# Queries and first expert groups of the latent routing as plain fp32 products, weights left unsplit, in a two-layer network on one core

## The chip, the cores and the metric

The kernel runs on one core of one Trainium2 chip. The metric is the device time of one execution in microseconds (us), from the device's own clock; lower is better. The runs of the kernel before took 4352.44 us in the median (3 runs, 4348.89 to 4359.93).

## The reference, cut to what matters

The program is a chain of mixers and feed-forward blocks on 256 latent rows and 256 context rows of width 1024. The part that the change touches is the expert layer, called twice on the latents (layers 0 and 1 of the second block):

```
def peer(x [256 x 1024], w_query, sub_keys, u, v):
    qry = (x @ w_query) as 8 heads x 2 halves x 128
    s   = qry . sub_keys            # 128 keys per head and half
    the 16 best of each half, their 256 sums, the 16 best of those
    idx, gate = expert numbers and softmax of the 16 best, per row and head
    act  = gelu(x . u[idx])         # 16384 experts, as 128 groups of 128
    return sum(gate * act * v[idx])
```

All of it is fp32 in the reference.

## The kernel before, in words

**Split products.** TensorE has a one-pass form for 32-bit operands of reduced precision (`fp32r`). To keep fp32 accuracy the kernel splits every operand x into hi = x rounded to that form (ACT, line 221) and lo = x - hi (VectorE "DVE" or GpSimd "POOL", line 222), and makes three products hi*hi, hi*lo and lo*hi (`mm3`, lines 224 to 228). Weights come as 512 KB loads into one of five raw buffers (`wraw`, tag of lines 355 and 356), and their parts go to five `whi` and four `wlo` buffers. `unit` (line 325) loads and splits a block of weights, `unit32` (line 342) loads it and leaves it unsplit. A product of unsplit fp32 operands shows in the trace as two matmul records, and a split product as three.

**The latent expert layer, `peer_lat` (line 2029), for each of two layers.**
1. `norm_T` (line 438) normalises the 256 rows, transposes them on TensorE into the tile `nfull`, and splits that into the pair `plhh`, `plhl` (named hT), 4 column blocks of 128 at a time.
2. `route` (line 1736), eight heads. For each: load 128 keys (`skT`), load and split two halves of query weights, 16 split products of 128x256 into PSUM, copy (`qry`, line 1752), four key products in plain fp32 (`at`, line 1757), copy (`tks`, line 1759), and four `top16` on DVE (lines 1829 to 1837). `skT` and the four scratch tiles `t16` of the `top16` of a head share one pool tag of four buffers (line 156, "s1").
3. `topk` (line 1768), twice, all on DVE: sums of the candidates (line 1787), 8 `top16`, and two look-ups (lines 1809 to 1811) over 128x1024 elements.
4. `build_G` (line 1926): 64 steps, each with DVE comparisons (lines 1954 and 1961), four plain fp32 products (line 1964) and a copy (line 1965), then stores of the gate matrix to DRAM.
5. The dense stretch: for each of 128 groups the split of u (on DVE) and of v (ACT, POOL), 24 products for x.u (128x256) and 12 of 128x512 for the sum over v, into PSUM (lines 2023 to 2025).

**The groups ahead.** Beside steps 2 to 4 the first `backlog` groups of step 5 have their x.u computed in advance (`ahead`, line 2083): 20 in layer 0 and 36 in layer 1. Each loads a 512 KB block of u (`dense_w`, line 1970), splits it with the lower part on POOL (since `a_mod` and `a_pool` are 1), makes 24 split products (`dense_u`, line 1981) and applies gelu.

**What sets the order.** The kernel is traced in program order, and a scheduler then orders each engine's queue by a simulated timeline: the earliest-written instruction whose inputs and buffers are ready goes first. `lockstep` and `idle` place the groups ahead behind the heads in program order (`u_lag` is 18 steps, and the eight heads are 16), but the scheduler lifts them forward where an engine is idle. In layer 0 the expert work of the context rows runs in the background: row gathers by POOL (line 1883) and weighted sums on DVE (lines 1906 and 1912).

Of the kernel before, what the change touches and what calls it, by code (L numbers as in the profile page):

```python
# [9 lines left out]
F32 = mybir.dt.float32  # L10
# [3 lines left out]
AF = mybir.ActivationFunctionType  # L14
# [6 lines left out]
P = 128  # L21
# [3 lines left out]
def ds(a, n):  # L25
    return slice(a, a + n)
# [72 lines left out]
class Builder:  # L99
# [242 lines left out]
    def unit32(self, ap, kk=KD):  # L342

        n = ap.n
        src = ap.parts(kk)
        nh = len(src)
        kh = kk // nh
        raws = []
        for i in range(nh):
            raws.append(self.w_raw()[:, :kh * n].rearrange("p (k c) -> p k c", k=kh))  # L350
            self.load(raws[i], src[i])
        self.tick()
        return Rows(raws, kh)

    def w_raw(self, name="wraw"):
        return self.pw.tile([P, 1024], F32, name=name, tag="wraw", bufs=self.n_raw)
# [78 lines left out]
        self.rstd(ss[:, 1:2], ss[:, 0:1], n)  # L435
        return ss[:, 1:2]

    def norm_T(self, x, ntile, gcol, sc, sh, hT, t0, pool, keep=None):
        nc = self.nc
        gs = self.t_([P, KD], "gs")  # L440
        nc.vector.scalar_tensor_tensor(gs, sc, 1.0, gcol, op0=ALU.add, op1=ALU.mult)
        xn = []
        for t in range(ntile):
            r = self.row_rstd(x[:, t], 1024)
            y = self.t_([P, 1024], "xn")
            nc.vector.tensor_scalar(y, x[:, t], r, None, op0=ALU.mult)
            xn.append(y)
        nt = ntile * P
        for k2 in range(0, KD, 4):
            whole = not isinstance(hT, tuple)  # L450
            full = hT[:, ds(k2, 4), ds(t0, nt)] if whole else self.t_([P, 4, nt], "nfull")
            for k1 in range(0, 4, 2):
                ps = self.ps_tr([P, 2, nt])
                for k in range(2):
                    for t in range(ntile):
                        nc.tensor.transpose(ps[:, k, ds(t * P, P)], xn[t][:, ds((k2 + k1 + k) * P, P)], self.ident)
                for k in range(2):
                    kk = k2 + k1 + k
# [43 lines left out]
class Block1:  # L502
# [101 lines left out]
    def out_res(self, yT, kt, W, gbc, x):  # L604
        nc = self.nc
        groups = [(k, min(KD, kt - k)) for k in range(0, kt, KD)]
        for cb in range(0, 1024, 512):
            ps = [self.ps_mm([P, 512], name="orp") for _ in range(2)]
            for gi, (k0, kk) in enumerate(groups):
                for h in range(2):  # L610
                    w = self.unit(W[k0 * P:(k0 + kk) * P, cb + h * 256:cb + h * 256 + 256], kk)
                    for t in range(2):
                        hv = (yT[0][:, ds(k0, kk)], yT[1][:, ds(k0, kk)])
                        self.xs(ps[t][:, ds(h * 256, 256)], hv, t * P, w, 0, 256, kk,
                                start=gi == 0 and h == 0, stop=gi == len(groups) - 1 and h == 1)
# [239 lines left out]
    def transp_split(self, y, nk, yT, nt, t0=0):  # L855

        nc = self.nc
        for k0 in range(0, nk, 2):
            ps = self.ps_tr([P, 2, nt * P])
            for k in range(2):  # L860
                for t in range(nt):
                    nc.tensor.transpose(ps[:, k, ds(t * P, P)], y[:, t, ds((k0 + k) * P, P)], self.ident)
            self.split(yT[0][:, ds(k0, 2), ds(t0, nt * P)], yT[1][:, ds(k0, 2), ds(t0, nt * P)], ps)

    def attn_tiles(self, pm):
        nc, A = self.nc, self.A
# [848 lines left out]
class Peer:  # L1715
# [2 lines left out]
    s_mod, s_pool = 4, 0  # L1718
    g_mul, g_mod = 0, 4
    mod_r, s_lag, s_eng = 0, 3, "DVE"  # L1720
    bg_r, bg_dense, bg_ahead, a_mod, a_pool, u_lag, u_route = 0.0, 1.4, 1.0, 1, 1, (18, 18), (18, 20)

    def peer_const(self):
        nc, pc = self.nc, self.pc
# [11 lines left out]
    def route(self, layer, hT, T, out):  # L1736


        nc, A = self.nc, self.A
        code, gate = T("code", [P, 2, 8, 16]), T("gate", [P, 2, 8, 16])  # L1740
        tk = T("tk", [P, 2, 2, 16, 16])
        v1, iu = tk[:, 0], tk[:, 1].bitcast(U32)
        sk = A["peer_sub_keys_2"][layer]
        for h in range(8):
            skT = self.t_([P, 2, P], "skT")
            self.load(skT, sk[h])
            w = self.unit(A["peer_w_query_2"][layer][:, h * 256:h * 256 + 256])
# [12 lines left out]
            for t in range(2):  # L1760
                for c in range(2):
                    self.top16(v1[:, t, 2 * h + c], iu[:, t, 2 * h + c], sc[:, t, c])
            yield
        out += [code, gate]
        for t in range(2):
            yield from self.topk(v1[:, t], iu[:, t], code[:, t], gate[:, t], T)
# [200 lines left out]
                yield  # L1967
            nc.sync.dma_start(self.d_G[:, :, ds(t0, n)], Gs)

    def dense_w(self, layer, g, D, pool=False):  # L1970

        u = self.w_raw("ur")
        self.load(u, self.A["peer_u_2_T"][layer, g])
        uh, ul = self.w_hi("uh"), self.w_lo("ul")
        self.split(uh, ul, u, pool)
        v = lambda t: t.rearrange("p (k c) -> p k c", k=8)
        D["uhl", g] = v(uh), v(ul)

    x_lead = 2

    def dense_u(self, layer, g, hT, D):

        nc = self.nc
        uh, ul = D.pop(("uhl", g))
        pa = self.psu.tile([P, 256], F32, name="pact", bufs=2)
        for k in range(8):
            self.mm3(pa, uh[:, k], ul[:, k], hT[0][:, k], hT[1][:, k], k == 0, k == 7)
        ge = self.pge.tile([P, 256], F32, name="ge", bufs=self.backlog[layer] + 2)
        nc.scalar.activation(ge, pa, AF.Gelu)  # L1989
        D[g] = ge  # L1990
# [38 lines left out]
    def peer_lat(self, layer, x, mod, gcol, fill=None):  # L2029

        nc = self.nc
        self.es_ps.close()
        B = self.backlog[layer]
        with ExitStack() as es:
# [5 lines left out]
            with ExitStack() as esr:  # L2040
# [1 line left out]
                self.n_mm, self.n_tr, self.n_at = 2, 1, 1  # L2042
                pr = self.pool(esr, f"rt{layer}", "right")
                self.lo_pat = "d"
                self.norm_T(x, 2, gcol, mod[:, 32:40, 0], mod[:, 24:32, 0], hT, 0, ph)
                gbc = self.gate_bc(mod, 5, 0, ph, "plg")
                res = []
                u = self.ahead(layer, hT, D)
                tag = lambda name: dict(tag="Gs", bufs=2) if name == "eq" else dict(tag=name, bufs=1)
                T = lambda name, shape: pr.tile(shape, F32, name=name, **tag(name))  # L2050
                fill = fill or iter(())
                self.bg_rate = self.bg_r if layer == 0 else 0.0
                self.lockstep(self.route(layer, hT, T, res), chain(islice(self.idle(), 8), self.spread(islice(fill, self.mod_r), 1)), chain(islice(self.idle(), self.u_lag[layer]), islice(u, self.u_route[layer])))
                self.bg_rate = 0.0
                self.lockstep(self.build_G(res[0], res[1], pr), self.spread(chain(u, fill), self.g_spread))
                for _ in fill:
                    pass
            self.psc = self.pool(es, f"psc{layer}", psum=True)
            pv = self.pool(es, f"pv{layer}", "right")
            pacc = self.pool(es, f"pacc{layer}", "right", psum=True)  # L2060
# [22 lines left out]
    def ahead(self, layer, hT, D):  # L2083
        n = self.backlog[layer]
        for g in range(n):
            for i in range(g + 1 if g else 0, g + 2):
                if i < n:
                    self.dense_w(layer, i, D, i % self.a_mod < self.a_pool)
            self.dense_u(layer, g, hT, D)
            self.bg(self.bg_ahead)  # L2090
            yield
# [204 lines left out]
```

## Time and profile before

| what | value |
|---|---|
| median of 3 runs | 4352.44 us |
| the profiled execution, its own time | 4345.28 us |
| its span, first to last instruction | 4343.6 us |
| mean granted TensorE clock | 0.894 of full |
| busy: TensorE, weight load, DVE, ACT, POOL | 81%, 73%, 70%, 45%, 49% |
| layer 0: heads, topk, `build_G`, dense | from 2221, 2314, 2402, 2546 us |
| layer 1: heads, topk, `build_G`, dense | from 3405, 3493, 3585, 3728 us |

Times inside the profile are counted from the start of its span. PE is TensorE's matmul and PEld its weight load. A matmul record lasts longer than the step to the next, since matmuls are pipelined, so the step between starts is what a product costs in a row of products.

### The profile page before, as it was taken

The numbers are of one execution on the slowest core, as the hardware profiler recorded it, in microseconds if no ns is written. First come the engines' busy times: TensorE is split into PE (matmuls) and PEld (weight loads), VectorE is DVE, ScalarE is ACT, GpSimd is POOL, SyncE is SP. The second block draws the span as 40 slices with busy tenths as digits, with TensorE's granted clock in tenths as the row PEclk, the third lists the DMA queues.
The fourth block names the chain that finished last, engine by engine and source line by source line (L and its number), as shares of the span: only waits on it lengthen the run. The fifth ranks groups of instructions, "written<-read, shape, count | busy, mean of one in ns | idle before, by whom it ended". The sixth has DMA issues, their size and how long they took to land. (4 is left out here: it accounts for less than half of the span.)

```text
span 4343.6 us, 68593 instructions
## 1 busy us (share of the span) xinstructions
PE 3525.7 (81%) x25277; PEld 3153.0 (73%) x25277; DVE 3039.7 (70%) x5920; ACT 1936.6 (45%) x3523; POOL 2126.1 (49%) x1632
## 2 busy tenths in 40 slices
PE   6788779697777864676586779999978878899998
PEld 4667768585677864566486668988857878799997
DVE  3745457876779986877668977888895599544435
ACT  3355444245344443244233345555545434455555
POOL 1233312453466764667716058888863161444444
PEclk8788889788888987888788999999999989999999
DMA  7586443663677887888755779999872345666655
GB/s 281 173 237 192 119 156 131 234 222 135 216 276 252 278 288 223 277 268 247 241 208 176 242 252 340 331 325 326 325 244 89 119 138 182 220 207 216 208 175 184
DMA packets 424010, 972.05 MB, mean 224 GB/s; under 512 B 70322, under 2 KB 211834, under 8 KB 418938
## 3 DMA queue, kind: packets, MB, share of 16 engines
q1 hardware_dynamic: 349946, 699.20, 49.4%
q0 software_dynamic: 73728, 268.47, 17.7%
q8 instruction: 199, 3.26, 0.3%
q14 instruction: 137, 1.12, 0.1%
HBM read 898.66 MB, written 68.88 MB: 223 GB/s over the span
## 5 line engine op out<-in xcount | busy, mean ns | idle before, releaser
L222 POOL TENSOR_TENSOR vl<-vr,vh 128x512 fp32r<-128x512 f32 x460 | 652.7, 1437 | 584.4 <-ACT vh L221 580.0
L226 PE MATMUL pact<-plhh,uh 128*128 128x256 f32 x2048 | 584.6, 285 | 31.4 <-ACT ge L1989 31.3
L227 PE MATMUL pact<-plhl,uh 128*128 128x256 f32 x2048 | 584.7, 285 | 0.0
L228 PE MATMUL pact<-plhh,ul 128*128 128x256 f32 x2048 | 584.5, 285 | 0.0
L221 ACT ACTIVATE whi<-wraw 128x1024 fp32r<-128x1024 f32 (+1 forms) x350 | 366.6, 1050 | 398.1 <-PE mm L227 115.0
L1883 POOL DMA_INDIRECT sg<-in_peer_u_dram,sidx x256 | 332.3, 1298 | 296.8 <-DVE sg L1906 190.0
L222 DVE TENSOR_TENSOR wlo<-wraw,whi 128x1024 fp32r<-128x1024 f32 (+1 forms) x256 | 327.7, 1284 | 181.8 <-ACT whi L221 89.4
L1912 DVE SCALAR_TENSOR_TENSOR spy<-sg,sact,spy 128x1024 f32<-128x1024 f32 x254 | 429.1, 1689 | 20.4 <-DMA sg<-in_peer_v_dram,sidx 19.1
L1883 POOL DMA_INDIRECT sg<-in_peer_v_dram,sidx x256 | 336.9, 1316 | 208.8 <-DVE spy L1912 113.4
L1906 DVE SCALAR_TENSOR_TENSOR sg<-sg,sph 128x1024 f32<-128x1024 f32 x256 | 381.3, 1500 | 79.0 <-DMA sg<-in_peer_u_dram,sidx 78.6
L2024 PE MATMUL acc<-vl,ch 128*128 128x512 f32 x1024 | 407.6, 398 | 26.7 <-POOL vl L222 18.3
L226 PEld LDWEIGHTS pact<-plhh,uh 128*128 128x128 f32 x2048 | 395.8, 193 | 42.8 <-ACT ge L1989 32.6
L227 PEld LDWEIGHTS pact<-plhl,uh 128*128 128x128 f32 x2048 | 395.7, 193 | 10.4
L2025 PE MATMUL acc<-vh,cl 128*128 128x512 f32 x1024 | 400.9, 391 | 0.0
L228 PEld LDWEIGHTS pact<-plhh,ul 128*128 128x128 f32 x2048 | 395.5, 193 | 4.3 <-POOL ul L222 0.2
L221 ACT ACTIVATE uh<-ur 128x1024 fp32r<-128x1024 f32 x256 | 271.1, 1059 | 264.0 <-PE pact L227 182.3
L2023 PE MATMUL acc<-vh,ch 128*128 128x512 f32 x1024 | 357.2, 395 | 30.1 <-ACT vh L221 30.1
L222 POOL TENSOR_TENSOR wlo<-wraw,whi 128x1024 fp32r<-128x1024 f32 (+1 forms) x94 | 233.2, 2491 | 298.1 <-PE mm L228 74.6
L221 ACT ACTIVATE vh<-vr 128x512 fp32r<-128x512 f32 x512 | 307.6, 624 | 117.5 <-PE acc L2025 100.2
L222 DVE TENSOR_TENSOR ul<-ur,uh 128x1024 fp32r<-128x1024 f32 x200 | 282.5, 1413 | 109.0 <-PE pact L228 104.7
L2004 DVE TENSOR_TENSOR cl<-co,ch 128x256 fp32r<-128x256 f32 x256 | 107.6, 420 | 217.7 <-ACT ch L2003 215.8
L2000 DVE TENSOR_TENSOR co<-co,G 128x256 f32<-128x256 f32 x256 | 167.3, 654 | 121.9 <-ACT co L1999 98.3
(647 smaller groups left out, 10116.7 us busy)
## 6 DMA issues: line engine op xcount, KB each, us to landing
ur<-in_peer_u_T_dram SPq DMA_DIRECT2D x256, 512.0 KB
vr<-in_peer_v_dram SPq DMA_DIRECT2D x256, 512.0 KB
wraw<-in_ada_w_dram SPq DMA_DIRECT2D x96, 512.0 KB
wraw<-in_dn_w_in_dram SPq DMA_DIRECT2D x96, 512.0 KB
wraw<-in_w_in_dram SPq DMA_DIRECT2D x64, 512.0 KB
d_G<-Gs SPq DMA_DIRECT2D x32, 1024.0 KB
G<-d_G SPq DMA_DIRECT2D x32, 1024.0 KB
wraw<-in_w_mod_dram SPq DMA_DIRECT2D x48, 512.0 KB
```

The source lines that it names most:

```text
L221: nc.scalar.activation(hi, src, AF.Copy)
L222: (nc.gpsimd if pool else nc.vector).tensor_tensor(lo, src, hi.bitcast(F32), ALU.subtract)
L226: mm(out, lh, rh, start=start, stop=False)
L227: mm(out, lh, rl, start=False, stop=False)
L228: mm(out, ll, rh, start=False, stop=stop)
L1883: nc.gpsimd.indirect_dma_start(out=g, out_offset=None, in_=A[tab][0], in_offset=bass.IndirectOffsetOnAxis(ap=self.s_idx[:, t, j:j + 1], ax ...
L1906: nc.vector.scalar_tensor_tensor(g, g, 1.0, h, op0=ALU.mult, op1=ALU.mult, accum_out=act[:, j:j + 1])
L1912: nc.vector.scalar_tensor_tensor(y, g, act[:, j:j + 1], y, op0=ALU.mult, op1=ALU.add)
L2000: nc.vector.tensor_tensor(co, co, D["G"][:, :, g % 8], ALU.mult)
L2023: mm(acc[t][h], ch[:, tt], vh[h], start=first, stop=False)
L2024: mm(acc[t][h], ch[:, tt], vl[:, hh], start=False, stop=False)
L2025: mm(acc[t][h], cl[:, tt], vh[h], start=False, stop=last)
```

## The change

It does four things, in `peer_lat` alone:
- `norm_T` writes the unsplit transposed rows into two tiles `plf` (named hf) taken from the four `wlo` buffers, instead of the scratch `nfull`. The pair hT is still split from it, for the dense stretch.
- `route` and `ahead` get hf instead of hT. So the queries and the groups ahead load their weights unsplit and make one plain fp32 product where three split products stood.
- While `wide` is 2 (from the norm to the end of `build_G`) unsplit loads take turns between the `wraw` and the `whi` buffers, ten instead of five.
- Groups ahead are loaded three ahead instead of one (`a_lead`), without any split.

Branches for an unsplit input are also added to `out_res` and `transp_split`; their callers still hand in pairs. The context's routing (`peer_ctx`) also hands in a pair. The core of the diff:

```diff
+    wide, wide_i = 1, 0
+    def raw32(self):
+        tags = (("wraw", self.n_raw), ("whi", self.n_hl), ("wlo", self.n_lo))[:self.wide]
+        self.wide_i += 1
+        tag, n = tags[self.wide_i % len(tags)]
+        return self.pw.tile([P, 1024], F32, name="wraw", tag=tag, bufs=n)
...
     def unit32(self, ap, kk=KD):
-            raws.append(self.w_raw()[:, :kh * n].rearrange("p (k c) -> p k c", k=kh))
+            raws.append(self.raw32()[:, :kh * n].rearrange("p (k c) -> p k c", k=kh))
...
     def norm_T(...):
-            full = hT[:, ds(k2, 4), ds(t0, nt)] if whole else self.t_([P, 4, nt], "nfull")
+            full = (hT if whole else plain)[:, ds(k2, 4), ds(t0, nt)] if whole or plain is not None else self.t_([P, 4, nt], "nfull")
...
     def route(...):
-            w = self.unit(A["peer_w_query_2"][layer][:, h * 256:h * 256 + 256])
+            w = (self.unit if isinstance(hT, tuple) else self.unit32)(A["peer_w_query_2"][layer][:, h * 256:h * 256 + 256])
...
-    def dense_w(self, layer, g, D, pool=False):
-        u = self.w_raw("ur")
+    def dense_w(self, layer, g, D, whole=False):
+        v = lambda t: t.rearrange("p (k c) -> p k c", k=8)
+        u = self.raw32() if whole else self.w_raw("ur")
         self.load(u, self.A["peer_u_2_T"][layer, g])
+        if whole:
+            D["u", g] = v(u)
+            return
...
     def dense_u(self, layer, g, hT, D):
         for k in range(8):
-            self.mm3(pa, uh[:, k], ul[:, k], hT[0][:, k], hT[1][:, k], k == 0, k == 7)
+            if isinstance(hT, tuple):
+                self.mm3(pa, u[0][:, k], u[1][:, k], hT[0][:, k], hT[1][:, k], k == 0, k == 7)
+            else:
+                nc.tensor.matmul(pa, u[:, k], hT[:, k], start=k == 0, stop=k == 7)
...
     def peer_lat(...):
-                self.norm_T(x, 2, gcol, mod[:, 32:40, 0], mod[:, 24:32, 0], hT, 0, ph)
+                hf = Rows([self.pw.tile([P, 4, 256], F32, name="plf", tag="wlo", bufs=self.n_lo) for _ in range(2)], 4)
+                self.norm_T(x, 2, gcol, mod[:, 32:40, 0], mod[:, 24:32, 0], hT, 0, ph, plain=hf)
+                self.wide = 2
...
-                u = self.ahead(layer, hT, D)
+                u = self.ahead(layer, hf, D)
...
-                self.lockstep(self.route(layer, hT, T, res), ...)
+                self.lockstep(self.route(layer, hf, T, res), ...)
...
+            self.wide = 1
...
     def ahead(self, layer, hT, D):
-            for i in range(g + 1 if g else 0, g + 2):
+            n_x = self.a_lead
+            for i in range(g + n_x if g else 0, g + n_x + 1):
                 if i < n:
-                    self.dense_w(layer, i, D, i % self.a_mod < self.a_pool)
+                    self.dense_w(layer, i, D, True)
```

## Rows read from the trace of the kernel before

**Rows 1.** Busy time by stretch: us, PE, PEld, DVE, ACT, POOL, PEclk, DMA share, GB/s.
```profile
2314.00:2402.00 88.00, 38.47 (x304) 36.70 (x302) 86.54 (x257) 17.48 (x28) 44.45 (x26) 0.74 0.52 168
...
2546.00:3140.00 594.00, 580.54 (x3616) 519.58 (x3617) 494.23 (x487) 316.65 (x621) 518.13 (x351) 1.00 0.90 327
3405.00:3493.00 88.00, 80.51 (x634) 78.65 (x632) 49.85 (x238) 40.30 (x55) 25.48 (x11) 0.95 0.46 139
3493.00:3585.00 92.00, 63.50 (x493) 62.89 (x492) 91.44 (x225) 32.15 (x46) 54.80 (x21) 0.85 0.38 124
3585.00:3728.00 143.00, 110.60 (x859) 103.88 (x858) 125.31 (x338) 58.19 (x95) 12.52 (x5) 0.95 0.62 188
3728.00:4300.00 572.00, 571.19 (x3472) 513.91 (x3473) 245.03 (x343) 324.04 (x645) 277.54 (x215) 0.99 0.62 208
```

**Rows 2.** Timeline of one head in layer 1: start us, us, engine, line, operation.
```profile
3473.55 0.60 ACT L1759 ACTIVATE tks<-at 128x512 f32<-128x512 f32 x1 [0.20 <-PE at L1757]
...
3474.18 0.87 DVE L1832 MAX8 tk<-tks 128x8 f32<-128x128 f32 x4 [4.74 <-ACT tks L1759]
...
3478.25 0.33 SPq L168 DMA_DIRECT2D skT<-in_peer_sub_keys_dram  x1
...
3481.51 1.06 PE L1757 MATMUL at<-skT,qry 128*128 128x128 f32 x8
...
3482.86 0.59 ACT L1759 ACTIVATE tks<-at 128x512 f32<-128x512 f32 x1
```

**Rows 3.** The score copies of the eight heads, layer 0 then layer 1.
```profile
L1759 ACT ACTIVATE tks<-at x8: 581/599/599, 2242.4 to 2313.7; 128x512 f32<-128x512 f32 x8
...
L1759 ACT ACTIVATE tks<-at x8: 581/597/599, 3424.6 to 3492.4; 128x512 f32<-128x512 f32 x8
```

**Rows 4.** Groups of 3405 to 3493: busy us, mean ns, idle before and releasers.
```profile
L226 PE MATMUL mm<-plhh,whi 128*128 128x256 f32 x128 | 37.9, 299 | 4.2 <-ACT plhh L221 2.2 <-ACT qry L1752 2.0
...
L226 PE MATMUL pact<-plhh,uh 128*128 128x256 f32 x60 | 17.1, 286 | 0.0
...
L222 DVE TENSOR_TENSOR wlo<-wraw,whi 128x1024 fp32r<-128x1024 f32 x12 | 14.6, 1216 | 9.0 <-PE mm L228 7.9 <-ACT whi L221 1.1
```

**Rows 5.** TensorE's timeline near 2303 us, layer 0.
```profile
2302.58 0.28 PE L226 MATMUL pact<-plhh,uh 128*128 128x256 f32 x1
2302.70 0.28 PE L227 MATMUL pact<-plhl,uh 128*128 128x256 f32 x1
...
2302.94 1.06 PE L1757 MATMUL at<-skT,qry 128*128 128x128 f32 x8
```

**Rows 6.** DVE's groups of the topk stretch of layer 1, 3493 to 3585.
```profile
L1809 DVE TENSOR_TENSOR eq<-tkpf,iotaf 128x1024 f32<-128x1024 f32 x4 | 13.6, 3436 | 0.1
L1810 DVE TENSOR_TENSOR eq<-eq,tk 128x1024 f32<-128x1024 f32 x4 | 11.3, 2860 | 0.0
...
L1810 DVE TENSOR_TENSOR eq<-eq,cand 128x1024 f32<-128x1024 f32 x4 | 8.7, 2202 | 0.0
L1787 DVE TENSOR_TENSOR cand<-tk 128x64 f32<-128x64 f32 (+3 forms) x10 | 7.9, 823 | 0.0
L1817 DVE SCALAR_TENSOR_TENSOR cand<-cand 128x128 f32<-128x128 f32 x2 | 4.9, 2448 | 0.1
L1809 DVE TENSOR_TENSOR eq<-tkpf,starts 128x1024 f32<-128x1024 f32 x4 | 4.7, 1218 | 0.0
L1774 DVE CAST tk<-tk 128x256 f32<-128x256 uint32 x2 | 4.0, 2022 | 0.0
...
L1818 DVE TENSOR_TENSOR tkpf<-tkpf,cand 128x128 f32<-128x128 f32 x2 | 0.6, 292 | 0.1
```

**Rows 7.** DVE's groups of the topk stretch of layer 0, 2314 to 2402.
```profile
L1787 DVE TENSOR_TENSOR cand<-tk 128x64 f32<-128x64 f32 (+3 forms) x10 | 8.0, 835 | 0.0
L1810 DVE TENSOR_TENSOR eq<-eq,cand 128x1024 f32<-128x1024 f32 x4 | 6.9, 1759 | 0.0
...
L1822 DVE TENSOR_TENSOR tkex<-tkb 128x128 f32<-128x128 f32 x2 | 2.7, 1350 | 0.0
```

More of the change, by code (lines that the diff above doesn't have):

```diff
@@ L436, in row_rstd, with norm_T @@
         return ss[:, 1:2]
-    def norm_T(self, x, ntile, gcol, sc, sh, hT, t0, pool, keep=None):
+    def norm_T(self, x, ntile, gcol, sc, sh, hT, t0, pool, keep=None, plain=None):
         nc = self.nc
@@ L610, in out_res @@
                 for h in range(2):
-                    w = self.unit(W[k0 * P:(k0 + kk) * P, cb + h * 256:cb + h * 256 + 256], kk)
+                    both = isinstance(yT, tuple)
+                    w = (self.unit if both else self.unit32)(W[k0 * P:(k0 + kk) * P, cb + h * 256:cb + h * 256 + 256], kk)
                     for t in range(2):
-                        hv = (yT[0][:, ds(k0, kk)], yT[1][:, ds(k0, kk)])
+                        hv = (yT[0][:, ds(k0, kk)], yT[1][:, ds(k0, kk)]) if both else yT[:, ds(k0, kk)]
                         self.xs(ps[t][:, ds(h * 256, 256)], hv, t * P, w, 0, 256, kk,
@@ L862, in transp_split @@
                     nc.tensor.transpose(ps[:, k, ds(t * P, P)], y[:, t, ds((k0 + k) * P, P)], self.ident)
-            self.split(yT[0][:, ds(k0, 2), ds(t0, nt * P)], yT[1][:, ds(k0, 2), ds(t0, nt * P)], ps)
+            if isinstance(yT, tuple):
+                self.split(yT[0][:, ds(k0, 2), ds(t0, nt * P)], yT[1][:, ds(k0, 2), ds(t0, nt * P)], ps)
+            else:
+                nc.scalar.activation(yT[:, ds(k0, 2), ds(t0, nt * P)], ps, AF.Copy)
     def attn_tiles(self, pm):
@@ L1720 @@
     mod_r, s_lag, s_eng = 0, 3, "DVE"
-    bg_r, bg_dense, bg_ahead, a_mod, a_pool, u_lag, u_route = 0.0, 1.4, 1.0, 1, 1, (18, 18), (18, 20)
+    bg_r, bg_dense, bg_ahead, u_lag, u_route = 0.0, 1.4, 1.0, (18, 18), (18, 20)
     def peer_const(self):
@@ L1968, in build_G @@
             nc.sync.dma_start(self.d_G[:, :, ds(t0, n)], Gs)
-    def dense_w(self, layer, g, D, pool=False):
-        u = self.w_raw("ur")
+    def dense_w(self, layer, g, D, whole=False):
+        v = lambda t: t.rearrange("p (k c) -> p k c", k=8)
+        u = self.raw32() if whole else self.w_raw("ur")
         self.load(u, self.A["peer_u_2_T"][layer, g])
+        if whole:
+            D["u", g] = v(u)
+            return
         uh, ul = self.w_hi("uh"), self.w_lo("ul")
[L1975 to L1979, printed above, removed]
+        self.split(uh, ul, u)
+        D["u", g] = v(uh), v(ul)
+    x_lead, a_lead = 2, 3
     def dense_u(self, layer, g, hT, D):
         nc = self.nc
-        uh, ul = D.pop(("uhl", g))
+        u = D.pop(("u", g))
         pa = self.psu.tile([P, 256], F32, name="pact", bufs=2)
         for k in range(8):
-            self.mm3(pa, uh[:, k], ul[:, k], hT[0][:, k], hT[1][:, k], k == 0, k == 7)
+            if isinstance(hT, tuple):
+                self.mm3(pa, u[0][:, k], u[1][:, k], hT[0][:, k], hT[1][:, k], k == 0, k == 7)
+            else:
+                nc.tensor.matmul(pa, u[:, k], hT[:, k], start=k == 0, stop=k == 7)
         ge = self.pge.tile([P, 256], F32, name="ge", bufs=self.backlog[layer] + 2)
@@ L2052, in peer_lat @@
                 self.bg_rate = self.bg_r if layer == 0 else 0.0
-                self.lockstep(self.route(layer, hT, T, res), chain(islice(self.idle(), 8), self.spread(islice(fill, self.mod_r), 1)), chain(islice(self.idle(), self.u_lag[layer]), islice(u, self.u_route[layer])))
+                self.lockstep(self.route(layer, hf, T, res), chain(islice(self.idle(), 8), self.spread(islice(fill, self.mod_r), 1)), chain(islice(self.idle(), self.u_lag[layer]), islice(u, self.u_route[layer])))
                 self.bg_rate = 0.0
```

## The prediction

> **What bounds the kernel now.** I read the split by stretch first, then the timeline and the groups of each stretch. The two dense stretches hold more than half of the span after 2221 us, and PE is busy there for 580.5 of 594 us and 571.2 of 572 us [rows 1]. The change leaves their products alone, so a dense stretch that begins earlier ends earlier by as much. What can move is the part ahead of each: heads, topk and `build_G`.
>
> In the heads neither DVE (49.9 of 88 us) nor POOL is full [rows 1]. One head costs a chain, seen whole in one turn [rows 2]: scores copied at 3473.55, `top16` from 3474.18, and the keys of the next head loaded only at 3478.25, since `skT` gets its buffer from the first scratch tile of that `top16`. Their key products start at 3481.51 and the next copy at 3482.86. A turn is 3482.86 - 3473.55 = 9.31 us, while DVE and ACT mostly wait. PE is busy for 80.5 of 88 us [rows 1], but part of that is group work lifted forward: 60 of the hi*hi products, so 60 / 8 = 7.5 groups [rows 4].
>
> In topk DVE is the bound: 91.4 of 92 us in layer 1 and 86.5 of 88 in layer 0, while POOL works for 54.8 and 44.5 us [rows 1]. Here the lengths matter more than the counts. The comparison of 128x1024 elements takes 1.22 us in one look-up and 3.44 us in the other, four of each, the same shape and operation [rows 6]. The slow ones stand where POOL makes lower parts of u. In `build_G` DVE is again the fullest, 125.3 of 143 us [rows 1].
>
> **The change, part by part.** *The product's price.* A split product steps by 2302.70 - 2302.58 = 0.12 us, so three cost 0.36 us [rows 5]. No plain fp32 product of 128x256 is in the trace. The nearest is the key product, 128x128 in two records: eight records in 1.06 us of which the last takes 0.28, so a step is (1.06 - 0.28) / 7 = 0.111 us, and a product 0.22 [rows 5]. With twice the columns it is at most 0.45 us if the step grows with the columns, and that I take, as the nearest row. The low end is 0.36 us (no dearer than now). The high end has no overlap between records: 0.28 + 0.11 for the second 128 columns, twice, 0.78 us.
>
> The Trainium skill, "Perfetto Trace Analysis", section Engine Utilization, puts the array at half its output rate for the two-part fp32 form; I estimate from it, at the full 2.4 GHz clock, 256 / 1.2 GHz = 0.21 us for such a product. The key products' row speaks against it, with 0.22 us for half as many columns. By the page PE would have less to do than now, and the two rivals below that rest on PE's load would fall away; by the row PE has more.
>
> *PE's load.* 704 products change (2 x 128 of queries, 56 x 8 of groups), each dearer by 0.45 - 0.36 = 0.09: 63 us more PE work in all, where PE has room. The room in layer 0's topk is 88 - 38.5 = 50 us [rows 1]. In layer 1 I check a floor: 128 + 288 products x 0.45 = 187, eight key products of four x 0.22 = 7, and 512 records of `build_G` x 0.111 = 57, in all 251 us. From the first query product at about 3405 this ends at 3656 without any gap, and some 3661 with 5 us lost at the start, where the second half of the rows is still to come. The sum below lets the dense stretch start at 3728 - 42 = 3686, so PE fits, by 25 us less the gaps that DVE leaves it.
>
> *The heads.* The 9.31 us chain stays: `top16`, key load, key products and copy are untouched. PE's share of a turn becomes 16 x 0.45 + 0.9 = 8.1 us, under 9.31. What goes are DVE's 12 lower parts of query weights of 1.22 us in this stretch [rows 4], which sit between the `top16` of the early heads. So each of the seven turns falls to 9.31: from 2313.7 - 2242.4 = 71.3 us to 65.2 in layer 0, and from 67.8 in layer 1 [rows 3], -6.1 and -2.6. At the start the queries no longer wait for the split of the rows, 2.2 us in layer 1 [rows 4]; I take -2.2 in each layer. The ACT and POOL halves of the splits lay under the waits of the chain in the heads, and their removal is costed at nothing there.
>
> *Topk.* With POOL's 56 splits gone the DVE operations have their uncontended lengths. Layer 1, with 1.2 us for 128x1024 and 0.29 for 128x128 as the reference [rows 6]: 13.6 - 4.7 = 8.9; 11.3 - 4.7 = 6.6; 8.7 - 4.7 = 4.0; the ten sums 7.9 - 10 x 0.29 = 5.0; 4.9 - 0.6 = 4.3; the two casts of 128x256, at most 0.6 each, 4.0 - 1.2 = 2.8. Together -31.6 us. Layer 0 [rows 7]: 8.0 - 2.9 = 5.1; 6.9 - 4.7 = 2.2; 2.7 - 0.6 = 2.1. Together -9.4; the background gathers stay on POOL. All of it lies on the path, since DVE is full. Bounds: nothing if something else slows those operations; and 55 us in layer 1 at most, POOL's whole time there [rows 1].
>
> *`build_G`.* Layer 1 still has POOL for 12.5 us at its start [rows 1]; I take half, -6, between 0 and -12.5.
>
> *Loads and buffers.* The number of loads and their bytes are unchanged. SP's queue is in order: query and u loads issue earlier, since ten buffers take them, and `skT` stands behind fewer loads that wait for a split. At 139 GB/s in the heads against 327 in the dense stretch of layer 0 [rows 1] there is room, so nothing. hf holds two of the four lower-part buffers until the last group ahead, so dense groups lifted into `build_G` find two; the cover is PE's own work there, and without it the first dense groups would wait a split of 1.22 us each, under 4 us a layer.
>
> *Sum.* Layer 0: -6.1 - 2.2 - 9.4 = -18. Layer 1: -2.6 - 2.2 - 31.6 - 6 = -42. Together -60 us. The profiled execution took 4345.3 us, so 4285; the median of the runs stands 7 us above it, so **4292 us**.
>
> **The rivals.** (1) *Groups stand ahead of the last heads.* If the scheduler lifts 7.5 groups in front of the last scores as now, PE has 8 x 8.1 + 7.5 x 3.6 = 92 us in the heads instead of 8 x (48 x 0.12 + 0.9) + 7.5 x 2.9 = 75, and the heads end 17 us later than now: layer 0 +17 - 9 = +8, layer 1 +17 - 32 - 6 = -21. Sum -13, 4339 us. For it: PE is nearly full there now [rows 1]. Against: the gap of a turn shrinks from 9.31 - 6.7 = 2.6 to 1.2 us, and only gaps are filled.
>
> (2) *Layer 0 gives its part back.* Its dense stretch has POOL at 518 and DVE at 494 of 594 us and DMA at 0.90 [rows 1]; if the background gathers pace it, an earlier start is not an earlier end, and -42 remains: 4310 us. Against: PE is at 0.98 there.
>
> (3) *Slower: the product is dearer.* With p as its price, layer 1's PE chain from 3405 is 416 p + 64 us. Now the dense stretch starts 323 us after 3405, so layer 1 stops gaining at p = 0.62. Layer 0's heads, some 92 us now, take 128 p + 12 (5 lost at the start) and so cost what they do now at 0.63, where its -9 of topk remain. Both layers together turn at 0.64. At the high end, 0.78, layer 1 is +65 and layer 0 112 - 92 - 9 = +11: 4428 us. For it: no such product has been seen here. Against: the steps of the key products, and 0.64 needs a step 40% longer than their columns give.
>
> (4) *More than forecast.* If more of POOL's time in topk is paid by DVE than the groups listed, and key loads land sooner behind fewer waiting loads: up to -95, 4257 us.
>
> That the change does not do what it says: the branches in `out_res` and `transp_split` are never taken, and context routing keeps its splits; but `route` and `ahead` do get hf, so I give no chance to no effect.
>
> **How the numbers follow.** Forecast 0.55, rival 1 0.15, rival 2 0.14, rival 3 0.10, rival 4 0.06. A change of 0.3%, 13 us, is about what a measurement of this kernel can tell from none. Faster: forecast, rivals 2 and 4, and half of rival 1, 0.82; within 0.3%: the other half, 0.08; slower: 0.10. The range, 4255 to 4340 us, holds all but rival 3 and the tails.
>
> **What would show it.** Right: 448 group products and 256 query products, each two records with a step near 0.225; no POOL lower part of u in the topk; the comparisons of line 1809 near 1.2 us throughout; layer 1's topk near 60 us instead of 92; turns of the heads near 9.3 us; the dense stretches starting about 18 and 60 us earlier. Wrong: a step well above 0.3; slow comparisons beside an idle POOL; more than four groups ahead of the last scores of a layer; gaps of PE in the dense stretch.

## The result, and the profile after

The changed kernel takes 4293.8 us (4285.2 to 4301.8, four runs) against 4350.7 us of the kernel before, measured beside it: a ratio of 0.9875, 95% interval 0.9856 to 0.9893. A later measurement gave 4301.6 against 4354.1 us, 0.9884 (0.9866 to 0.9902); one of its six executions took 5201 us at a granted clock of 0.64, and the ratio leaves that one out. The forecast was 4292 us. The total agrees; the terms do not, and this section shows which.

The profiled execution of after took 4301.8 us, 8 above its median; that of before was 5 under its own. So the two traces differ by 43.5 us where the medians differ by 57.

Busy time by stretch after (us, then PE, PEld, DVE, ACT, POOL, PEclk, DMA share, GB/s), to be laid beside [rows 1]: layer 0's heads, topk, `build_G` and dense stretch, then layer 1's start, heads, topk, `build_G` and dense stretch.

```profile
2221.00:2316.00 95.00, 95.00 (x478) 84.10 (x477) 35.87 (x226) 19.12 (x36) 0.00 (x0) 1.00 0.46 147
2316.00:2390.00 74.00, 39.92 (x191) 33.00 (x189) 72.47 (x260) 9.41 (x18) 18.78 (x17) 0.79 0.64 214
2390.00:2535.00 145.00, 105.98 (x806) 89.98 (x806) 126.65 (x359) 55.26 (x91) 2.08 (x2) 0.94 0.69 212
2535.00:3128.00 593.00, 583.12 (x3645) 523.82 (x3646) 491.01 (x491) 319.74 (x627) 522.46 (x354) 1.00 0.91 330
3378.00:3400.00 22.00, 21.17 (x97) 17.91 (x98) 3.33 (x4) 7.80 (x13) 0.55 (x1) 0.84 0.24 74
3400.00:3479.00 79.00, 79.00 (x394) 70.29 (x394) 33.41 (x224) 13.26 (x27) 0.00 (x0) 1.00 0.48 155
3479.00:3532.00 53.00, 53.00 (x247) 46.65 (x246) 52.08 (x222) 11.94 (x22) 0.00 (x0) 1.00 0.48 151
3532.00:3686.00 154.00, 124.75 (x848) 113.87 (x846) 121.24 (x342) 55.70 (x95) 0.00 (x0) 0.97 0.62 185
3686.00:4256.00 570.00, 569.76 (x3470) 512.55 (x3471) 243.34 (x341) 324.11 (x644) 277.03 (x215) 1.00 0.62 209
```

POOL is at 0 in layer 1 from the heads to the dense stretch, and layer 1's topk is 53 us long instead of 92. But PE is busy without a gap through both heads and layer 1's topk. In the heads it is the bound now. In topk it is not: DVE works there for 52.1 of 53 us. The heads are longer, as the score copies of both layers show beside [rows 3]:

```profile
L1773 ACT ACTIVATE tks<-at x8: 597/597/597, 2236.9 to 2315.8; 128x512 f32<-128x512 f32 x8
...
L1773 ACT ACTIVATE tks<-at x8: 597/597/597, 3400.0 to 3478.8; 128x512 f32<-128x512 f32 x8
```

A turn is 78.8 / 7 = 11.26 us in the mean in both layers, where 9.31 was forecast. Timeline of one turn in layer 1 and, first, of a run of query products at layer 0's start (start us, us, engine, line, operation; other lines left out):

```profile
2226.27 9.72 PE L383 MATMUL mm<-plf,wraw 128*128 128x256 f32 x44
...
3444.36 1.05 PE L1771 MATMUL at<-skT,qry 128*128 128x128 f32 x8
3445.26 1.89 PE L383 MATMUL mm<-plf,wraw 128*128 128x256 f32 x8
3445.45 0.60 ACT L1773 ACTIVATE tks<-at 128x512 f32<-128x512 f32 x1 [7.43 <-PE at L1771]
3446.98 3.62 PE L2007 MATMUL pact<-plf,wraw 128*128 128x256 f32 x16
3450.10 0.33 SPq L168 DMA_DIRECT2D skT<-in_peer_sub_keys_dram  x1
3450.44 5.34 PE L383 MATMUL mm<-plf,wraw 128*128 128x256 f32 x24
3455.62 1.05 PE L1771 MATMUL at<-skT,qry 128*128 128x128 f32 x8
```

The keys are still loaded 4.65 us behind the score copy, as in [rows 2]. But between two score products stand a group, 3450.44 - 3446.98 = 3.46 us, and 8 + 24 = 32 query records: with the scores' 0.9 us PE's own work fills the turn. The mixture differs from turn to turn: the first two hold 46 and 50 query records and next to no group work, the last holds three groups and no query. In all nine groups stand ahead of the last scores of each layer.

DVE's groups in layer 1's topk, 3479 to 3532, beside [rows 6]: what took 13.6, 11.3 and 8.7 us takes 4.7 each.

```profile
L1823 DVE TENSOR_TENSOR eq<-tkpf,iotaf 128x1024 f32<-128x1024 f32 x4 | 4.7, 1221 | 0.1
L1824 DVE TENSOR_TENSOR eq<-eq,tk 128x1024 f32<-128x1024 f32 x4 | 4.7, 1219 | 0.0
...
L1824 DVE TENSOR_TENSOR eq<-eq,cand 128x1024 f32<-128x1024 f32 x4 | 4.7, 1218 | 0.0
...
L1831 DVE SCALAR_TENSOR_TENSOR cand<-cand 128x128 f32<-128x128 f32 x2 | 0.6, 294 | 0.1
```

The stages of every kernel of this study, from the timelines: start (first copy of normalized rows to first score copy), heads (to the last score copy), topk (to the first `gi`, the tile that `build_G` begins with), `build_G` (to the last copy of a step's gate products, `Gs`), us; last the median of its runs.

| kernel | layer 0 | layer 1 | time |
|---|---|---|---|
| before | 25.8, 71.2, 88.8, 130.5 | 23.4, 67.8, 91.7, 131.2 | 4350.7 |
| after | 17.1, 78.8, 74.2, 132.2 | 19.4, 78.8, 53.2, 140.9 | 4293.8 |
| e1 POOL back | 19.2, 78.8, 77.1, 132.9 | 19.4, 79.0, 65.6, 142.1 | 4318.3 |
| e2 queries only | 17.1, 77.8, 89.7, 130.9 | 17.1, 79.3, 92.1, 129.7 | 4345.5 |
| e3 groups only | 19.0, 77.8, 74.3, 131.6 | 19.0, 77.2, 53.2, 141.0 | 4324.2 |
| e4 heads first | 17.1, 68.4, 73.8, 128.6 | 17.1, 68.3, 53.2, 165.1 | 4308.0 |
| e5 POOL twice | 17.1, 79.6, 81.8, 131.3 | 19.1, 79.7, 85.2, 144.7 | 4344.8 (one run) |
| e6 own keys | 17.1, 52.4, 75.9, 132.4 | 17.1, 52.4, 53.2, 160.8 | 4276.0 (one run) |
| e7 transposes first | 19.1, 78.8, 74.5, 130.6 | 19.3, 78.8, 53.2, 143.0 | 4299.2 (one run) |
| e8 before, own rows | 19.4, 68.7, 89.1, 130.6 | 20.3, 69.0, 91.4, 132.7 | 4340.8 (one run) |
| e9 own keys, timed | 17.1, 52.5, 74.6, 135.4 | 17.1, 52.4, 53.2, 161.0 | 4274.5 |
| e10 after again | 17.1, 78.8, 74.5, 131.6 | 19.3, 78.8, 53.2, 140.9 | 4301.6 |
| e11 e9 and e7 | 17.1, 52.4, 74.0, 133.3 | 17.1, 52.4, 53.2, 160.9 | 4271.7 |
| e12 before, own keys | 26.3, 45.9, 102.5, 129.5 | 23.4, 45.9, 91.1, 144.4 | 4328.9 |

Before to after, layer 0: start -8.7, heads +7.6, topk -14.6, `build_G` +1.7, together -14.0. Layer 1: -4.0, +11.0, -38.5, +9.7, together -21.8. The rest of the traces' -43.5 lies outside: +3.1 ahead of layer 0's first row copy, -10.0 between layer 0's last `Gs` copy and layer 1's first row copy, -1.1 behind. The dense stretches (first `acc` product) begin at 2535.4 instead of 2545.9 and at 3686.2 instead of 3728.8 us: 10.5 and 42.6 us earlier, where about 18 and 60 were to show the forecast right.

### The profile page after: what moved, and what is told of

It is laid out like the page before. It is cut to its first block, busy times and chain, and to the rows that moved or that the text cites. A ratio compares the mean times of both kernels' runs of the same rounds, so it can differ in the third digit from the quotient of the medians.

```text
span 4300.1 us, 66834 instructions
## 1 busy us (share of the span) xinstructions
PE 3555.2 (83%) x24573; PEld 3149.5 (73%) x24573; DVE 2938.3 (68%) x5888; ACT 1851.1 (43%) x3435; POOL 1978.6 (46%) x1576
## 4 chain that ended last, share of the span: by engine, by line
PE 41%; DVE 13%; DMA 7%; issue 5%; POOL 4%; ACT 2%; SPq 0%; POOLq 0%; DVEq 0%; ACTq 0%
PE acc L2044 5%; PE acc L2043 5%; PE acc L2045 5%; PE pact L228 4%; PE pact L227 4%; PE pact L226 4%; PE pact L2007 4%; PE mm L383 3%; DVE gA L1975 2%; DVE sg L1920 2%; DMA wraw<-in_dn_w_in_dram 2%; DMA cRB<-d_rowsl 1%; POOL sg L1897 1%; DVE spy L1926 1%; DVE gB L1968 1%
## 5 line engine op out<-in xcount | busy, mean ns | idle before, releaser
L221 ACT ACTIVATE whi<-wraw 128x1024 fp32r<-128x1024 f32 (+2 forms) x318 | 332.8, 1049 | 337.5 <-DMA wraw<-in_dn_w_in_dram 83.9
L226 PE MATMUL pact<-plhh,uh 128*128 128x256 f32 x1600 | 453.7, 284 | 1.5 <-ACT uh L221 1.5
L228 PE MATMUL pact<-plhh,ul 128*128 128x256 f32 x1600 | 454.2, 284 | 0.0
L227 PE MATMUL pact<-plhl,uh 128*128 128x256 f32 x1600 | 454.1, 284 | 0.0
L1926 DVE SCALAR_TENSOR_TENSOR spy<-sg,sact,spy 128x1024 f32<-128x1024 f32 x254 | 421.2, 1658 | 20.5 <-DMA sg<-in_peer_v_dram,sidx 19.3
L1920 DVE SCALAR_TENSOR_TENSOR sg<-sg,sph 128x1024 f32<-128x1024 f32 x256 | 379.9, 1495 | 77.8 <-DMA sg<-in_peer_u_dram,sidx 77.2
L2044 PE MATMUL acc<-vl,ch 128*128 128x512 f32 x1024 | 407.3, 398 | 20.3 <-POOL vl L222 13.5
L222 DVE TENSOR_TENSOR wlo<-wraw,whi 128x1024 fp32r<-128x1024 f32 (+2 forms) x224 | 290.5, 1302 | 150.2 <-ACT whi L221 90.5
L222 POOL TENSOR_TENSOR wlo<-wraw,whi 128x1024 fp32r<-128x1024 f32 (+1 forms) x94 | 233.2, 2490 | 300.9 <-PE mm L228 68.4
L226 PEld LDWEIGHTS pact<-plhh,uh 128*128 128x128 f32 x1600 | 306.7, 192 | 11.0 <-ACT uh L221 1.6
L227 PEld LDWEIGHTS pact<-plhl,uh 128*128 128x128 f32 x1600 | 306.6, 192 | 10.2
L228 PEld LDWEIGHTS pact<-plhh,ul 128*128 128x128 f32 x1600 | 306.6, 192 | 4.2 <-DVE sg L1920 0.4
L221 ACT ACTIVATE uh<-ur 128x1024 fp32r<-128x1024 f32 x200 | 212.0, 1060 | 197.3 <-PE pact L227 185.0
```

Of the source, the lines that this page charges most:

```text
L221: nc.scalar.activation(hi, src, AF.Copy)
L222: (nc.gpsimd if pool else nc.vector).tensor_tensor(lo, src, hi.bitcast(F32), ALU.subtract)
L226: mm(out, lh, rh, start=start, stop=False)
L227: mm(out, lh, rl, start=False, stop=False)
L228: mm(out, ll, rh, start=False, stop=stop)
L1920: nc.vector.scalar_tensor_tensor(g, g, 1.0, h, op0=ALU.mult, op1=ALU.mult, accum_out=act[:, j:j + 1])
```

## The experiments

The theory after the comparison: (a) topk gained because POOL left DVE alone; (b) the heads lost because groups stand in the turns of a full PE; (c) the start gained from the rows' buffers; (d) `build_G` of layer 1 lost because its transposes stand behind groups. The rivals are named with each.

**e1 and e5: POOL's work put back.** In `dense_w`, one multiplication by a column of ones (e5: two) for each group ahead; the product still reads unsplit u. Here and below only the lines that matter of each edit are shown.

```diff
         if whole:
+            self.nc.gpsimd.tensor_tensor(u, u, self.one.to_broadcast([P, 1024]), ALU.mult)
             D["u", g] = v(u)
```

> The changed kernel with one POOL multiplication of 128x1024 by one put back for each of the 56 groups ahead; PE, ACT, loads and buffers stay as they are. Theory (the topk gained because POOL no longer works beside DVE): layer 1's topk returns from 53 to 85-92 us, layer 0's from 74 to 84-89, with look-up comparisons near 3.4 us beside POOL work; layer 1's build_G falls back from 141 to about 131, since PE has time to work off its groups; in all 30 to 40 us above the changed kernel, about 4330. Rival (the topk gained from something else, such as shorter waits for ACT's exponential or fewer splits on ACT): topk stays at 53 and 74 within 4 us, total within 6 us of 4294.

> As e1, with two POOL multiplications for each group ahead instead of one, so that POOL works nearly without pause (2 x 1.89 us for each group of 3.45 us). Theory (DVE's two-input operations are held for as long as POOL works, and what they lose depends on POOL's pauses: 0.69 us for each us of POOL in the kernel before, where the pauses were 0.5 us, 0.39 in e1, where they were 1.6): look-up comparisons at 3 us or more, layer 1's topk 85 to 110 us, layer 0's above 80. Rival (a fixed price for each POOL operation): comparisons near 2.1 us and layer 1's topk near 53 + 2 x 12.4 = 78 us, layer 0's near 80.

Layer 1's topk took 65.6 us in e1 and 85.2 in e5. So the contention is real: 12.4 of the 38.5 us come back in e1 and 32.0 in e5; in layer 0, where the gain was 14.6, they are 3 and 7.6. But e1 fell short of its 85, and e5's look-ups were not the slow part, so each expectation is half missed. Another part of e1's failed whole: `build_G` of layer 1 was to fall back to 131, and took 142.1 (144.7 in e5). PE made no more of its groups in the longer topk (243 and 256 records, 247 in after) and waited there for 10.6 and 24.4 us for a gelu on ACT. The trace of e5 shows what the contention costs (POOL, then DVE, near the second look-up of layer 1):

```profile
3524.58 26.63 POOL L1993 TENSOR_TENSOR wraw<-wraw,one 128x1024 f32<-128x1024 f32 x14 [12.57 <-DMA wraw<-in_peer_u_T_dram]
3563.01 10.41 POOL L1993 TENSOR_TENSOR wraw<-wraw,one 128x1024 f32<-128x1024 f32 x5 [11.80 <-DMA wraw<-in_peer_u_T_dram]
...
3528.91 9.26 DVE L1803 TENSOR_TENSOR cand<-tk 128x128 f32<-128x128 f32 x5
...
3559.70 2.36 DVE L1825 TENSOR_TENSOR eq<-tkpf,iotaf 128x1024 f32<-128x1024 f32 x2
3561.98 4.05 DVE L1826 TENSOR_TENSOR eq<-eq,tk 128x1024 f32<-128x1024 f32 x2
```

POOL waits for loads from 3551.2 to 3563.0, and the comparisons of 3559.70 take 2.36 us for two. POOL resumes, and the next two take 4.05. While POOL ran back to back, the five small sums took 9.26 / 5 = 1.85 us each, one POOL operation (26.63 / 14 = 1.90) for every sum. So what DVE pays is about one POOL operation for each of its own that meets one: the number of meetings counts, not their size. The Trainium skill, "SBUF — State Buffer", section "SBUF: two separate sides", states a rule that fits this for VectorE operations with two SBUF inputs beside a GpSimd operation that reads SBUF: whichever starts first takes a shared pair of ports for the whole instruction, and the other "fully blocks". The `TENSOR_REDUCE` of 128x1024, one input, kept its 1.2 us in all these kernels; this agrees. One input alone is no safeguard: in e5's topk a `COPY` of 128x8 took 1.69 us and a `CAST` of 128x128 1.64, against 0.15 and 0.23 in after. In e1 POOL paused 1.6 us between operations, and fewer meetings cost 12.4 us. In before the pauses were 0.5 us and the operations 2.4 us long. The original two-input subtraction was not put back alone, and 6.5 us of layer 1's gain did not return.

**e2 and e3: one part alone.** In e2 `ahead` gets the split rows and the groups their splits again, lower parts on POOL, one load ahead; in e3 `route` gets the split rows and the queries their splits. Both keep the five raw buffers of before (`wide` stays 1) and hold one half of the unsplit rows in a buffer of its own.

```diff
-                u = self.ahead(layer, hf, D)
+                u = self.ahead(layer, hT, D)
```

```diff
-self.route(layer, hf, T, res)
+self.route(layer, hT, T, res)
```

> Only the queries are plain products; the groups ahead keep their splits, lower parts on POOL, one load ahead, five raw buffers (one of the two row halves lies in a buffer of its own). Theory (the queries give the start and cost the heads, and nothing in topk): start 19 and 22 us as in the changed kernel (28 and 26 before), turns of the heads 16 x 0.43 + 0.9 + one split group of 2.9 = 10.7 us, topk 89 and 92 as before, build_G 130 in both; sum -9 -4 +4 +7 = about -2 against before, 4349. Rival (as forecast: turns fall to 9.3 when DVE's lower parts of the query weights go): -13 against before, 4338.

> Only the groups ahead are plain products; the queries keep their splits (three lower-part buffers instead of four, since one holds half of the rows). Theory: start 28 and 26 us as before; turns 48 x 0.12 + 0.9 + 3.45 = 10.1 us; topk 74 and 53 as in the changed kernel; build_G of layer 1 about 137; sum -15 -38 +3 +6 = about -44 to -50 against before, 4300 to 4306. Rival (the groups' part alone brings little because the queries' splits on DVE and ACT hold it up): less than -25, over 4325.

e2: 4345.5 us, a ratio of 0.9979 (0.9963 to 0.9996). Topk stays as before, the start gains, the heads lose: turns 11.1 and 11.3 us with split groups between them. e3: 4324.2 us, 0.9938 (0.9914 to 0.9963), less than expected. Its stages are after's within 2 us a layer, its topk to 0.1. So by the stages the gain is the groups': -37 us in e3, -36 in after, +3 in e2. By the times it is not so clean: e2 lies 8 us and e3 29 below the kernel before, after 52 to 57. In e3's trace what is missing lies in layer 0's dense stretch, 710.9 us from first to last `acc` product (the sum over v) against 686.5 in after; why is open. And its start was 19.0 us although its queries wait for the split, which led to e8.

**e8: the rows alone.** On the kernel before, the rows' second half gets a tile of its own.

```diff
-            full = hT[...] if whole else self.t_([P, 4, nt], "nfull")
+            full = hT[...] if whole else own if own is not None and k2 else self.t_([P, 4, nt], "nfull")
```

> The kernel before with one edit: the second half of the latents' rows, ahead of the split, lies in a tile of its own instead of a scratch tile that waits for the split of the first half. Theory (most of the start's gain comes from the rows' buffers, so that the transposes of the second half no longer stand behind 22 query products): from the first row copy to the first score copy 19 us in each layer instead of 25.8 and 23.4; heads, topk and build_G as before; total about -11, 4340. Rival (the split itself, now off the queries' path, gives the gain): the start stays within 2 us of 25.8 and 23.4.

Start 19.4 and 20.3 us: -6.4 and -3.1 of the -8.7 and -4.0. The row copies of e8:

```profile
2220.40 1.02 ACT L459 ACTIVATE nfull<-tr,mod,gs 128x256 f32<-128x256 f32 x2 [0.75 <-PE tr L456]
2221.45 1.06 ACT L221 ACTIVATE plhh<-nfull 128x1024 fp32r<-128x1024 f32 x1
2222.63 1.02 ACT L459 ACTIVATE nown<-tr,mod,gs 128x256 f32<-128x256 f32 x2
2224.86 1.02 ACT L459 ACTIVATE nown<-tr,mod,gs 128x256 f32<-128x256 f32 x2 [1.21 <-PE tr L456]
```

and of before:

```profile
2219.93 1.06 ACT L221 ACTIVATE plhh<-nfull 128x1024 fp32r<-128x1024 f32 x1
2222.34 1.02 ACT L459 ACTIVATE nfull<-tr,mod,gs 128x256 f32<-128x256 f32 x2 [1.35 <-DVE plhl L222]
2227.13 1.02 ACT L459 ACTIVATE nfull<-tr,mod,gs 128x256 f32<-128x256 f32 x2 [3.77 <-PE tr L456]
```

Before, the third copy waits for DVE's lower part, which reads the scratch tile it needs, and the last transposes then stand behind query products on PE: the fourth copy comes 4.79 us after the third, in e8 2.23. Part of e8's gain is the clock: TensorE's granted clock was 0.50 to 0.54, the level of 1.2 GHz, in 2217 to 2226 and again in 2229 to 2236 of before, behind stretches in which PE waited, and in e8 up to 2227 and not again.

**e4: the heads ahead of all groups.** `self.scored` is the last score product of the eighth head.

```diff
-            self.dense_u(layer, g, hT, D)
+            with self.tc.issue_after(self.scored):
+                self.dense_u(layer, g, hT, D)
```

> The changed kernel with every product of the groups ahead ordered behind the scores of the eighth head on PE. Theory (PE is full in the heads because one group of 3.45 us stands in each turn): turns fall from 11.3 to the chain's 9.3 us, heads from 79 to 65 us in both layers; layer 0's topk has room for the groups (PE 40 of 74 us), so layer 0 gains 10 to 14 us; layer 1 has PE full through topk and hands its 9 groups on to build_G, so it gains 0 to 5; in all -10 to -18, about 4280. Rival (the load of the next head's keys sets the turn of 11.3): turns stay within 0.4 of 11.3 and the total within 5 us or above, the groups only standing later.

Turns fall to 68.4 / 7 = 9.77 us; the third to fifth take 9.30 each, and in the last two PE waits 6.9 us for the keys. So the key chain was still there, hidden under a full PE. Layer 0 gains as expected (start to last `Gs` copy 302.3 to 287.9 us), but layer 1 does not hold: its heads' 10 us come back as 24 in `build_G`. The heads, topk and `build_G` of layer 1 in e4:

```profile
3374.00:3443.00 69.00, 51.54 (x254) 45.49 (x253) 33.41 (x224) 7.87 (x15) 0.00 (x0) 0.91 0.39 119
3443.00:3496.00 53.00, 51.78 (x239) 45.18 (x238) 52.15 (x223) 13.41 (x24) 0.00 (x0) 0.99 0.46 140
3496.00:3662.00 166.00, 154.31 (x1001) 141.52 (x999) 119.59 (x336) 58.15 (x101) 0.00 (x0) 1.00 0.61 181
```

PE idles for 17 us in the heads and then has 154 us of work in `build_G`: 4308.0 us, 0.9901 (0.9877 to 0.9926), not better than after. The trace is of e4's fastest execution, 4290.7 us, so its stages do not explain that median.

**e6 and e9: keys in buffers of their own.** `self.pr` is the stage's pool; the key load no longer waits for a scratch tile.

```diff
-            skT = self.t_([P, 2, P], "skT")
+            skT = self.t_([P, 2, P], "skT") if isinstance(hT, tuple) else self.pr.tile([P, 2, P], F32, name="skT", bufs=2)
```

> The changed kernel with two buffers of their own for the keys, so that their load waits for no scratch tile. Theory (PE is full in the heads: 6.9 + 0.9 + 3.45 us a turn): keys are loaded earlier, turns stay at 11.3 us within 0.2, total within 8 us of 4294. Rival (the key load sets the turn, as forecast): turns fall by over 0.6 us, total by 5 us a layer.

> The kernel of e6 again, timed. Theory (a planner that sees each head's scores wait for its keys fills the wait with a group, and without the wait it does not): turns 7.5 us with one group ahead of the last scores, as in e6; layer 0 gains 24 us and layer 1 some 8, so 18 to 33 us below the changed kernel in this call. Rival (e6 was one lucky execution): less than 10 us below it.

e6 went against my theory: a turn is 7.49 us, and one group instead of nine stands ahead of the last scores. In e9 again, layer 1:

```profile
3394.29 0.33 SPq L168 DMA_DIRECT2D skT<-in_peer_sub_keys_dram  x1
...
3401.90 7.07 PE L383 MATMUL mm<-plf,wraw 128*128 128x256 f32 x32
3402.09 0.33 SPq L168 DMA_DIRECT2D skT<-in_peer_sub_keys_dram  x1
3408.81 1.05 PE L1771 MATMUL at<-skT,qry 128*128 128x128 f32 x8
3409.96 0.60 ACT L1773 ACTIVATE tks<-at 128x512 f32<-128x512 f32 x1 [5.05 <-PE at L1771]
```

A key load stands right behind the scores that free its buffer; with two buffers it brings the keys of the head after next. Those of the scores at 3408.81 were loaded at 3394.29, 14.5 us ahead, and PE runs 32 query records and the scores, no group. So both readings held one half. In after PE's work sets the turn, but the group stands there only as long as the order was planned with a wait for the keys. How the planner weighs it is in no trace; that the groups go when the wait goes is shown by e6, e9 and e12. e9: 4274.5 us, 0.9821 (0.9803 to 0.9839), 27 us below after measured beside it (e10). Layer 0's stages are 22 us shorter than e10's and layer 1's 8, as expected.

> The changed kernel, unedited, for comparison: 4294 us within 6, turns 11.3, topk 74 and 53, build_G 132 and 141 within 2 us each; layer 0's dense stretch 685 to 690 us if its 686.5 against 693.8 before is the change's, 693 or above in some executions if it varies by itself.

The stages came as expected, and layer 0's dense stretch took 688.6 us; the time, 4301.6 us, is 2 above the range.

**e7 and e11: `build_G`'s transposes ahead of groups.** `self.turned` is the last transpose. e7 on after, from group 24; e11 on e9, from group 16, with 16 groups in `route` and the rest of layer 1's placed closer together.

```diff
-            self.dense_u(layer, g, hT, D)
+            with self.tc.issue_after(self.turned) if layer == 1 and g >= 24 else nullcontext():
+                self.dense_u(layer, g, hT, D)
```

> The changed kernel with groups 24 to 35 of layer 1 ordered behind build_G's last transpose on PE. Theory (build_G grew from 131 to 141 us since its three transposes each stand behind some 4.75 us of group records): the last gT copy comes at most 7 us after the first gi instead of 12.2, the first Gs copy at most 12 instead of 18, and build_G takes 134 to 137 us. Rival (PE's total sets the end of build_G): the first Gs copy comes earlier, but the last stays within 2 us of 141 after the first gi.

> e9 with groups 16 to 35 of layer 1 ordered behind build_G's last transpose (16 groups in route instead of 20, three instead of four ticks between the rest). Theory (PE is full in layer 1 from the queries to the last G product, 148 of 160 us in e6's build_G): the last gT copy comes under 7 us after the first gi instead of 16.8, but the last Gs copy gains no more than the 12 us of PE's gaps; build_G 150 to 158 us instead of 161, total 0 to 10 below e9. Rival (the transposes set build_G's end): build_G falls by 11 us or more, to 150 or less.

Waits in `build_G` of layer 1, in after (us in total, times, longest; `gT` are the transposed tiles, `gA` a step's comparisons):

```profile
DVE gT L1957 <- PE tr L1955: 9.5, 3, 4.5
...
DVE gA L1975 <- PE mm L1978: 7.6, 4, 1.9
```

and in e7, where the first of the two has gone from the list:

```profile
DVE gA L1976 <- PE mm L1979: 15.3, 7, 4.1
```

The last `gT` copy came 3.8 us after the first `gi` instead of 12.2, the first `Gs` copy 11.8 instead of 18.0, and still `build_G` took 143.0 us: the wait moved to the G products. In e11, the same on e9, `build_G` took 160.9 us. Busy time of that stretch in e11, columns as above:

```profile
3485.00:3647.00 162.00, 151.69 (x982) 139.28 (x982) 120.28 (x337) 57.85 (x99) 0.00 (x0) 0.98 0.61 180
```

PE works for 152 of 162 us. The rival of e7 holds: earlier transposes do not end `build_G` earlier, and (d) falls. That PE's total ends it, with its 10 us of waits, is the reading left. e11's 4271.7 us (0.9808, 0.9789 to 0.9827) is not told apart from e9. These two are the fastest kernels here.

**e12: own keys in the kernel before.** The same edit, latents only.

> The kernel before with the keys in two buffers of their own, the queries and groups split as they were. Theory (the key load makes the wait that the planner fills, in the kernel before as well): turns fall from 10.2 and 9.7 to 48 x 0.12 + 0.9 = 6.7 to 7.5 us, with at most 3 groups ahead of the last scores instead of 7; heads 47 to 53 us; topk as before or longer by up to 10 us, since POOL's splits for the groups then all fall into it; total 20 to 38 below before. Rival (before, the splits of the query weights set the turn): turns stay above 9 us.

Turns 45.9 / 7 = 6.56 us. 25 us come out of layer 0's heads and 22 out of layer 1's; 13.7 return in layer 0's topk and 13.2 in layer 1's `build_G`. 4328.9 us, 0.9942 (0.9921 to 0.9963). The two changes add: -25 here, -52 for after measured beside it (e10), -80 for e9.

## Why the prediction was right, and where it was not

*Price of a product.* 16 records take 3.45 us, so a product costs 0.431 us, against 0.45 taken. Rival 3, which turns at 0.64, is out. A nearer row than the key products stood in the trace of before: line 1083 makes unsplit products of 128x64 by 128x256, the same 256 columns; eight of its records take 1.94 us, the last 0.38, so a record steps by 0.22, and a product of two by 0.45. The Trainium skill's "Perfetto Trace Analysis", section Engine Utilization, weighed in the prediction with 0.21 for a product, is not borne out. Another, the Trainium skill, "FP8 and Floating Point Precision", section "TensorE Precision Notes", counts four passes for true fp32; my estimate from it at 2.4 GHz, 4 x 256 / 2.4 = 0.427 us, agrees with the trace.

*Heads, -6.1 and -2.6 forecast, +7.6 and +11.0 measured.* This step failed: "So each of the seven turns falls to 9.31." Rival 1's mechanism came true in its place, with nine groups ahead of the last scores, not 7.5. The argument against it, that only gaps are filled and 1.2 us is left of them, took the gap in the trace for the gap in the plan; that the plan saw a longer one is argued from e6, e9 and e12, where the groups go with the key wait, and stands in no trace. The chain itself was read well: with the groups held back it gave the 9.30 us of e4's middle turns.

*Start, -2.2 each forecast, -8.7 and -4.0 measured.* I costed the split's own time and missed the buffer: the diff's own tiles for the rows end the wait of the second half, and with it transposes behind query products. e8 shows that part, -6.4 and -3.1, with the clock's share in it. The clock is also part of why layer 0 gained more than layer 1: with the same code the start took 17.1 us where the granted clock was 1.00 (layer 0 of after, both layers of e2) and 19.2 to 19.4 where it was 0.84 to 0.87 (layer 1 of after, both of e1).

*Topk, -9.4 and -31.6 forecast, -14.6 and -38.5 measured.* Right in mechanism (e1, e5), short in size: the list left out groups that met POOL too, `gate` and `code` the largest, 3.8 and 2.8 us in before and 0.6 each in after. This is the first half of rival 4. For layer 0 it is shown for about half of the gain, 7.6 us in e5. Layer 1's 53 us lies under the "near 60" that was to show it.

*`build_G` of layer 1, -6 forecast, +9.7 measured.* The step "so PE fits" failed. Its floor on PE left 25 us "less the gaps that DVE leaves it", and three rows of after use up 46. PE's groups in `build_G`, and the stretch behind it:

```profile
L1978 PE MATMUL mm<-gB,gA 128*128 128x128 f32 x512 | 72.6, 282 | 16.2 <-DVE gA L1975 16.2
L226 PE MATMUL pact<-plhh,uh 128*128 128x256 f32 x48 | 14.3, 298 | 0.0
...
3673.00:3686.00 13.00, 0.00 (x0) 0.00 (x0) 2.17 (x5) 2.03 (x5) 0.00 (x0) 0.62 0.75 254
```

PE waits 16 us for DVE's comparisons. Six dense groups (48 / 8) are lifted into `build_G`, 3 x 48 split records at 0.12, so 17 us; they stood there in before too, and the floor did not count them. And PE is idle for the 13 us between the last gate product and the first dense one. So PE did not fit, and topk's surplus went here: with all that came ahead of it the second dense stretch began 42.6 us earlier, not 60.

*Loads, costed at nothing*: nothing in the stages contradicts it, but e2 and e3 took the ten buffers away only together with one of the parts, so their share is not shown. *Layer 0's part, rival 2*: not given back. Its dense stretch was even shorter, 686.5 us against 693.8 in before; eight more profiles of kernels with both parts took 685 to 689, and those with one part or none 690 to 711. Whether the change does this was not tried.

So the total is right by terms that offset, and partly by luck. Against the forecast the heads cost 13.7 + 13.6 = 27.3 us more and `build_G` 1.7 + 15.7 = 17.4 more; start and topk gave 8.3 and 12.1 us more. By the stages the gain is 60 - 44.7 + 20.4 = 36 us, not 60. The medians' 57 come with 8 us from outside the stages, whose cause is open, and 13 from where the two profiled executions lie among their runs.

## What to carry to other kernels

When work moves to an engine that is nearly full, add up that engine's whole stage with its gaps, and ask what a planned order will put into each wait: the cheapest gain here was two buffers of 1 KB a partition that removed the wait. A contended operation is priced by how often it meets the other engine, so small operations count as much as large ones. A tile of its own that ends a wait can be worth more than the arithmetic that a change saves.

## What the runs showed of the hardware

A POOL multiplication with one full tensor and one broadcast column took 1.89 us for 128x1024, the subtraction of two tensors 2.40. An fp32 product's two records stepped by 0.216 us each at a granted clock of 1.00. TensorE's granted clock was 1.00, the level of 2.4 GHz, in the start of layer 0 in after (2217 to 2237), with PE busy for 18.6 of 20 us. In before it was 0.70 in 2214 to 2242, a mean of both levels: it stood at 1.2 GHz (0.50 to 0.54) in 2217 to 2226, after PE had been busy for 2.3 of 4 us (2213 to 2217), and again in 2229 to 2236, after 1.1 of 3 us at 1.00 (2226 to 2229). At 1.2 GHz a split record stepped by 0.21 us instead of 0.12.
